# Attention logits over three PSUM banks, the third shared with the transposes

## The chip, the cores and the metric

The kernel runs on one core of one Trainium2 chip. The metric is the device time of one execution in microseconds (us); lower is better. The median of three runs of the kernel before is 2956.0 us (2955.72 to 2957.67).

## The reference

A decoder trunk of two layers over one sequence of 16 learned and 1024 given tokens (1040 rows of 1024 numbers): a state-space mixer and a gated feed-forward network (FFN), then attention and a second FFN. The change lies in the attention, which is of the stick-breaking kind, with 16 heads of 64:

```python
logits = jnp.einsum('bthd,bshd->bhts', q[:, t0:t1], k[:, :t1]).astype(jnp.float32) * scale
...
visible = s_idx < t_idx
log_keep = jnp.where(visible, jax.nn.log_sigmoid(-logits), 0.0)
later = lax.cumsum(log_keep, axis=3, reverse=True) - log_keep
log_w = jnp.where(visible, jax.nn.log_sigmoid(logits) + later, -jnp.inf)
w = jnp.exp(log_w).astype(v.dtype)
outs.append(jnp.einsum('bhts,bshd->bthd', w, v[:, :t1]))
```

Each weight is a sigmoid of its logit times the product of all sigmoids of the negated logits of later visible keys. The kernel computes that product directly, as a running product from right to left.

## The kernel before

The 16 heads go in eight pairs, p = 0 to 7. The 1040 tokens are nine chunks of 116 (the last has 112), and three chunks make a stretch of 348. A pair has 18 steps: step n is one chunk i of queries against one stretch jj of keys, for i = 0 to 8 and, within i, from the stretch that holds i down to the first. In the attention TensorE, VectorE, ScalarE and GpSimd run in the order in which the code is written; the code after it is ordered by a scheduler that works with simulated times.

One step, in the code's order:

- `weigh` (L1288): for both heads (a = 0, 1) a tile of logits `lg` in a PSUM bank, two products each (L1303). Then ScalarE makes from each tile the sigmoid of the negated logits, `kp` (L1306), and the plain sigmoid, `bt` (L1307), in the order kp0, bt0, kp1, bt1. A tile of logits is free after its `bt`. Where the stretch holds the query's own chunk (here jj = i // 3), GpSimd masks both (L1312). VectorE runs the product scan over `kp` (L1316) and multiplies it into `bt` (L1317).
- `place` (L1259): at steps 1, 3 and 9 the values of a stretch are turned on TensorE into a bank `pv` (L1267); VectorE evicts them to `v` (L1269), behind the scans of the step.
- `half` (L1209): half of a projection of 348 tokens, 12 products into a bank `pj` (L154 to L156). Steps 0 to 7 project for the pair itself, steps 8 to 17 for the next pair; the last pair has nothing there. Keys are evicted by VectorE (`k`, L1226), queries by ScalarE and VectorE (`qs`, L1250 and L1254), one step after their second half.
- pieces of the next weights' splitting (L1204 on ScalarE, L1205 on VectorE).
- `flush` (L1369): after every two chunks and after the last one of a pair the products with the values into a bank `po` (`values`, L1345; ScalarE evicts them as `o`, L1352), and in every step the transposes of the weights `bt` of three steps ago (`turn`): two banks `wT` (L1330), one for each head, evicted by ScalarE (L1334).

PSUM has eight banks, and four groups share them:

```python
def mm(self, s="mm"):
    return self.mp.tile([P, 512], F32, tag="mm", name=self.nm(s))
def sm(self, s="sm"):
    return self.sp.tile([P, 512], F32, tag="sm", name=self.nm(s))
def lg(self, s="lg"):
    return self.sp.tile([P, 512], F32, tag="lg", name=self.nm(s), bufs=LGB)
def ex(self, s="ex"):
    return self.sp.tile([P, 512], F32, tag="ex", name=self.nm(s), bufs=1)
```

`mm` has two banks (`pj`), `sm` three (`pv`, `wT`), `lg` two, `ex` one (`po`). A new tile gets a bank of its group when the tile that was in it has been read for the last time; within a group the allocator chooses the bank when the program is built. So before the change the tile of head a waits for `bt` of the same head in the step before.

## Time and profile before

| what | value |
|---|---|
| median of three runs | 2956.0 us |
| the profiled execution's own time | 2956.52 us |
| its span, first to last instruction | 2954.8 us |
| mean granted clock of TensorE | 0.988 |
| first and last logits of the attention | 1606.8 and 2130.4 us |
| products of logits (L1303) | 576, of 217 to 418 ns |

A profile row has the start and the length in us, engine, line, operation, tiles and shapes, and how many instructions it puts together; in brackets stands the idle time before it and the instruction that ended it. Products overlap on TensorE, so the pace is read from start to start. PE is TensorE, PEld its weight load, DVE VectorE, ACT ScalarE, POOL GpSimd.

### The profile page before, as it was taken

Reading aid. Unit: us, or ns where it says so; the run is one execution under the profiler, and the core shown is the slowest. Engines: PE = TensorE matmul, PEld = TensorE weight load, DVE = VectorE, ACT = ScalarE, POOL = GpSimd, SP = SyncE. Lnnn points to the kernel's source line nnn. Section 1 sums busy time; section 2 is a strip of 40 time slices with the busy share of each in tenths; the row PEclk is TensorE's granted clock in tenths of the full one; section 3 lists DMA queues with packets and bytes.
Section 4 is the critical chain, followed back from the end, with each engine's and each line's share of the span. In section 5 each row is a group of like instructions: output and inputs, shape, how many; then the busy total and the mean of one; then the engine's idle time right before and its main releaser. Section 6 shows DMA issues by size and latency. Waiting matters only on the chain.

```text
span 2954.8 us, 57105 instructions
## 1 busy us (share of the span) xinstructions
PE 2856.8 (97%) x21837; PEld 2723.3 (92%) x21837; DVE 2151.9 (73%) x4194; ACT 1616.9 (55%) x3302; POOL 962.6 (33%) x1088
## 2 busy tenths in 40 slices
PE   7999999989998999999999999999898999999998
PEld 4999898879998999999999999999798999999888
DVE  5686868885568565658986888888858656567895
ACT  4555545553236555555334888878726555555442
POOL 1253434440003666660002222222200666662000
PEclk9999999999999999999999999999999999999999
DMA  5233333324131222226242222222341222225331
GB/s 165 76 106 89 107 93 104 102 71 144 58 105 55 80 75 78 80 87 207 61 138 75 60 60 64 64 62 60 99 149 51 89 84 74 79 83 188 107 107 58
DMA packets 128962, 272.75 MB, mean 92 GB/s; under 512 B 15888, under 2 KB 59536, under 8 KB 128688
## 3 DMA queue, kind: packets, MB, share of 16 engines
q1 hardware_dynamic: 123376, 258.17, 27.7%
q10 hardware_dynamic: 4048, 6.36, 0.6%
q0 software_dynamic: 1264, 4.57, 0.4%
q8 instruction: 172, 2.82, 0.4%
q14 instruction: 102, 0.84, 0.1%
HBM read 200.93 MB, written 53.21 MB: 86 GB/s over the span
## 4 chain that ended last, share of the span: by engine, by line
PE 77%; DVE 12%; ACT 4%; issue 3%; DMA 2%; POOL 2%; SPq 0%; DVEq 0%; ACTq 0%; POOLq 0%
PE p L154 10%; PE p L155 10%; PE p L156 10%; PE acc L155 8%; PE acc L156 8%; PE acc L154 8%; PE pj L154 5%; PE pj L155 5%; PE pj L156 5%; PE po L1345 2%; PE lg L1303 2%; PE wT L1330 1%; DVE kp L1316 1%; DVE D L574 1%; ACT kp L1306 1%
## 5 line engine op out<-in xcount | busy, mean ns | idle before, releaser
L154 PE MATMUL pj<-uh,wh 128*128 128x348 f32 (+2 forms) x1536 | 506.9, 330 | 15.5 <-DVE qs L1254 7.2
L155 PE MATMUL pj<-ul,wh 128*128 128x348 f32 (+2 forms) x1536 | 498.7, 325 | 0.0
L156 PE MATMUL pj<-uh,wl 128*128 128x348 f32 (+2 forms) x1536 | 496.2, 323 | 0.0
L155 PE MATMUL p<-bl,fh 128*128 128x262 f32 (+1 forms) x1408 | 402.0, 286 | 4.1 <-DVE bl L837 4.1
L154 PE MATMUL p<-bh,fh 128*128 128x262 f32 (+1 forms) x1408 | 401.5, 286 | 3.2 <-ACT ft L937 2.3
L156 PE MATMUL p<-bh,fl 128*128 128x262 f32 (+1 forms) x1408 | 399.9, 285 | 0.2 <-DVE fl L890 0.2
L154 PEld LDWEIGHTS pj<-uh,wh 128*128 128x128 f32 x1536 | 291.8, 190 | 22.7 <-DVE qs L1254 9.3
L155 PE MATMUL p<-bl,wh 128*128 128x262 f32 (+1 forms) x1056 | 301.9, 286 | 6.7 <-DVE bl L837 6.7
L154 PE MATMUL p<-bh,wh 128*128 128x262 f32 (+1 forms) x1056 | 302.0, 286 | 3.4 <-ACT ft L937 1.8
L156 PE MATMUL p<-bh,wl 128*128 128x262 f32 (+1 forms) x1056 | 301.3, 286 | 0.0
L155 PEld LDWEIGHTS pj<-ul,wh 128*128 128x128 f32 x1536 | 292.5, 190 | 1.4 <-issue 0.5
L156 PEld LDWEIGHTS pj<-uh,wl 128*128 128x128 f32 x1536 | 291.6, 190 | 0.3 <-issue 0.2
L890 POOL TENSOR_TENSOR fl<-x,fh 128x1024 fp32r<-128x1024 f32 x80 | 192.6, 2408 | 251.8 <-ACT fh L889 251.8
L155 PEld LDWEIGHTS p<-bl,fh 128*128 128x128 f32 x1408 | 268.5, 191 | 6.0 <-DVE bl L837 5.7
L154 PEld LDWEIGHTS p<-bh,fh 128*128 128x128 f32 x1408 | 268.9, 191 | 4.6 <-ACT ft L937 2.8
L277 DVE SCALAR_TENSOR_TENSOR c<-p,params,c 128x260 f32<-128x260 f32 (+1 forms) x440 | 208.0, 482 | 89.0 <-ACT c L273 86.8
L156 PEld LDWEIGHTS p<-bh,fl 128*128 128x128 f32 x1408 | 267.7, 190 | 0.5 <-DVE fl L890 0.4
L940 DVE TENSOR_TENSOR p<-p,ft 128x262 f32<-128x262 f32 (+1 forms) x176 | 76.7, 437 | 215.5 <-ACT ft L937 123.8
L155 PE MATMUL acc<-gl,wh 128*128 128x260 f32 (+1 forms) x672 | 211.3, 320 | 0.1
L155 PEld LDWEIGHTS p<-bl,wh 128*128 128x128 f32 x1056 | 202.4, 192 | 7.7 <-DVE bl L837 7.7
L156 PE MATMUL acc<-gh,wl 128*128 128x260 f32 (+1 forms) x672 | 208.6, 320 | 0.0
L154 PEld LDWEIGHTS p<-bh,wh 128*128 128x128 f32 x1056 | 202.1, 192 | 4.3 <-ACT ft L937 2.5
(327 smaller groups left out, 7948.3 us busy)
## 6 DMA issues: line engine op xcount, KB each, us to landing
w<-in_w_up SPq DMA_DIRECT2D x88, 512.0 KB
w<-in_w_down SPq DMA_DIRECT2D x44, 512.0 KB
w<-in_w_in SPq DMA_DIRECT2D x40, 512.0 KB
E<-ea_d SPq DMA_DIRECT2D x32, 464.0 KB
D<-acs_d SPq DMA_DIRECT2D x32, 420.5 KB
g<-c SPq DMA_DIRECT2D x88, 130.0 KB
g<-c SPq DMA_DIRECT2D x88, 128.0 KB
b<-g SPq DMA_DIRECT2D x16, 520.0 KB
```

The lines of the kernel that those rows point to most:

```text
L154: mm(out, wh, uh, start=first, stop=False, skip_group_check=joins)
L155: mm(out, wh, ul, start=False, stop=False, skip_group_check=joins)
L156: mm(out, wl, uh, start=False, stop=last, skip_group_check=joins)
L277: nc.vector.scalar_tensor_tensor(to, ps[:, o + i : o + i + n], wcol(i), out, op0=ALU.mult, op1=ALU.add)
L574: nc.vector.tensor_scalar(dk[:, i], dk[:, i], self.cols[:n, 1, cc, h0 + i : h0 + i + 1], 0.0, op0=ALU.subtract, op1=ALU.min)
L890: tt(lo[:, :n], t, hi[:, :n].bitcast(F32), op=ALU.subtract)
L940: add = lambda o, x, y: tt(o[:, :N], x[:, :N], y[:, :N], op=ALU.add)
L1303: nc.tensor.matmul(ps[:nt, :m], part[:, c0 : c0 + nt], ks[a][:, s0 : s0 + m], start=x == 0, stop=x == 1)
L1306: nc.scalar.activation(kp[:nt, :m], ps[:nt, :m], AF.Sigmoid, scale=self.rt[2][:nt, i : i + 1])
L1316: nc.vector.tensor_tensor_scan(rev, rev, self.one[:nt].to_broadcast([nt, m + 1]), init, ALU.mult, ALU.mult)
L1330: nc.tensor.transpose(pt[:ns, x * CB : x * CB + nt], bt[a][:nt, x * CB : x * CB + ns], self.ident[:nt, :nt])
L1345: nc.tensor.matmul(po[64 * a : 64 * a + 64, w], v[: CH[c][1], c, 64 * a : 64 * a + 64], wt[a][: CH[c][1], c, :nt], start=x == 0, stop=x == ...
```

## The change

The tiles of logits take turns over a cycle of three calls, two of `lg` and one of `sm`. The cycle starts once for the attention; with 18 steps of two tiles each it stands alike in every pair. At steps 0, 3, 6 and so on both tiles are in `lg`; at steps 1, 4, 7, 10 and so on the first head's is in `sm`; at steps 2, 5, 8 and so on the second head's.

```diff
-            ps = self.lg()
+            ps = next(self.logits)("lg")
...
         turns, ready, wts, os, late, chores = [], [], {}, {}, [], []
+        self.logits = cycle((self.lg, self.lg, self.sm))
```

No instruction is added or taken away, and within the attention none changes its place on its engine. What changes is the tile that was in the bank before, and so what TensorE waits for. In the built program, from the second pair on:

| tile | waits for, before | waits for, after |
|---|---|---|
| second logits of a step | `bt1` of the step before | mostly `bt0` of the step before; at step 2 the first `wT` copy of step 1 |
| first logits of a step | `bt0` of the step before | tiles two steps back; at steps 4 and 10 the eviction of the `pv` of the step before |
| `pv` of step 1 | a `wT` copy of step 17 | the copy of the first `wT` of step 0 |
| `wT` | `wT` copies of the steps before, or `pv` | the same kind, or logits' `bt` |

TensorE from the last transposes of step 9 to the logits of step 10, in the fourth pair (`wT` transposes, `lg` logits, `qs` and `k` their operands):

```order
 L1330 MATMUL wT_21402<-ident,bt_21164 116x116 [waits Activation_49]
 L1330 MATMUL wT_21402<-ident,bt_21164 116x116 x2
-L1303 MATMUL lg_21410<-k_19989,qs_21061 116x348 [waits Activation_49]
+L1303 MATMUL lg_21410<-k_19989,qs_21061 116x348 [waits DVE_49,PE_49]
 L1303 MATMUL lg_21410<-k_19989,qs_21061 116x348
 L1303 MATMUL lg_21416<-k_19990,qs_21063 116x348 [waits Activation_49]
```

The first logits of step 10 stand where they stood, and wait for VectorE (the eviction of step 9's `pv`) instead of ScalarE.

TensorE at step 1 of the same pair, the logits and then `pv`:

```order
-L1303 MATMUL lg_20849<-k_19989,qs_20477 116x232 [waits Activation_49]
+L1303 MATMUL lg_20849<-k_19989,qs_20477 116x232 [waits PE_49]
 L1303 MATMUL lg_20849<-k_19989,qs_20477 116x232
 L1303 MATMUL lg_20855<-k_19990,qs_20479 116x232 [waits Activation_49]
 L1303 MATMUL lg_20855<-k_19990,qs_20479 116x232
-L1267 MATMUL pv_20874<-ident,v_20745 116x128 [waits PE_49]
+L1267 MATMUL pv_20874<-ident,v_20745 116x128 [waits PE_49,Activation_49]
```

The first logits no longer wait for ScalarE, and `pv` does.

Behind the attention the scheduler puts a few instructions of the second FFN's projection up in another order (some forty rows on TensorE, ten on VectorE and on ScalarE; SyncE and GpSimd keep theirs). TensorE there (`p` the sums, `bh` and `bl` the parts of the input, `fh` and `fl` of the weights):

```order
 L155 MATMUL p_27810<-bl_26764,fh_27734 128x258
 L156 MATMUL p_27810<-bh_26763,fl_27735 128x258
-L154 MATMUL p_27826<-bh_27392,fh_27734 128x258
-L155 MATMUL p_27826<-bl_27393,fh_27734 128x258
-L156 MATMUL p_27826<-bh_27392,fl_27735 128x258
-L154 MATMUL p_27826<-bh_27392,fh_27734 128x258
-L155 MATMUL p_27826<-bl_27393,fh_27734 128x258
 L154 MATMUL p_27635<-bh_27382,fh_26991 128x258
```

Five products of one sum moved behind a group of another sum; four of them now stand 12 rows later, behind that group, and the fifth some 50 rows later.

## The prediction

> **What bounds the kernel now.** I read the busy shares first, then the attention alone in the table by windows, then the waits of TensorE there, and last the timelines of one pair of heads around each wait. All steps below (0 to 17) are of the pair that starts at 1806.36 us; the pairs repeat every 67.4 us (step 0 of the next one stands at 1873.76).

> ```profile
> PE 2856.8 (97%) x21837; PEld 2723.3 (92%) x21837; DVE 2151.9 (73%) x4194; ACT 1616.9 (55%) x3302; POOL 962.6 (33%) x1088
> ...
> 1826.00:1879.00 53.00, 51.12 (x430) 48.47 (x430) 49.18 (x97) 45.08 (x128) 10.90 (x52) 1.00 0.27 73
> ...
> PE lg L1303 <- ACT bt L1307: 8.5, 24, 0.6
> PE pj L154 <- DVE qs L1254: 7.2, 7, 1.0
> ```

> TensorE is the kernel's bound as a whole. In the attention the table's columns (length; busy time of PE, PEld, DVE, ACT, POOL; granted clock) show two engines near their limit from step 4 to the next step 0: PE 51.1 and DVE 49.2 of 53 us. The last two rows are what TensorE waits for: the logits for ScalarE's second sigmoid (8.5 us in 24 waits), and once in each of seven pairs a projection for VectorE's `qs` (1.0 us). Only the first kind is a wait for a bank of the logits.

> VectorE has no room between these two points. It starts when ScalarE hands it step 4, runs on without a pause, and pauses again only before step 1 of the next pair:

> ```profile
> 1825.92 0.94 DVE L1316 TENSOR_TENSOR_SCAN kp<-kp,kp,one 116x349 f32<-116x349 f32 x1 [2.61 <-ACT kp L1306]
> ...
> 1846.86 0.61 DVE L1269 TENSOR_TENSOR v<-pv,rt 116x256 f32<-116x256 f32 x2
> ...
> 1848.86 0.94 DVE L1316 TENSOR_TENSOR_SCAN kp<-kp,kp,one 116x349 f32<-116x349 f32 x1
> ...
> 1866.96 1.07 DVE L1254 TENSOR_TENSOR qs<-pj,qs 64x348 fp32r<-64x348 f32 x2
> ```

> So the times of VectorE's rows between step 4 and step 16 are fixed relative to step 4, whatever TensorE gains in between. That decides which gains are kept.

> **What the change removes.** Three waits for logits' banks per pair, at steps 0, 8 and 12. TensorE's rows, each stalled place with one of the same width that isn't stalled (steps 3, 2 and 1):

> ```profile
> 1806.36 0.39 PE L1303 MATMUL lg<-k,qs 128*116 128x116 f32 x2
> 1807.15 0.41 PE L1303 MATMUL lg<-k,qs 128*116 128x116 f32 x2 [0.40 <-ACT bt L1307]
> 1807.40 0.38 PE L154 MATMUL pj<-uh,wh 128*128 128x348 f32 x1
> ...
> 1813.13 0.66 PE L1303 MATMUL lg<-k,qs 128*116 128x232 f32 x4
> 1813.63 0.49 PE L1267 MATMUL pv<-ident,v 128*116 128x128 f32 x3
> ...
> 1816.37 0.88 PE L1303 MATMUL lg<-k,qs 128*116 128x348 f32 x4
> 1817.08 0.32 PE L154 MATMUL pj<-uh,wh 128*128 128x344 f32 x1
> ...
> 1819.46 0.60 PE L1303 MATMUL lg<-k,qs 128*116 128x116 f32 x4
> 1819.90 0.52 PE L1267 MATMUL pv<-ident,v 128*116 128x128 f32 x3
> ...
> 1836.86 1.25 PE L1303 MATMUL lg<-k,qs 128*116 128x348 f32 x4
> 1837.94 0.32 PE L154 MATMUL pj<-uh,wh 128*128 128x348 f32 x1
> ...
> 1845.03 0.87 PE L1303 MATMUL lg<-k,qs 128*116 128x348 f32 x4
> ...
> 1851.33 0.45 PE L1303 MATMUL lg<-k,qs 128*116 128x232 f32 x2
> 1852.10 0.47 PE L1303 MATMUL lg<-k,qs 128*116 128x232 f32 x2 [0.32 <-ACT bt L1307]
> 1852.41 0.33 PE L154 MATMUL pj<-uh,wh 128*128 128x348 f32 x1
> ...
> 1866.18 0.87 PE L1303 MATMUL lg<-k,qs 128*112 128x348 f32 x4
> 1868.09 0.42 PE L154 MATMUL pj<-uh,wh 128*128 128x348 f32 x1 [1.03 <-DVE qs L1254]
> ```

> From the first product of the logits to what follows: step 0 takes 1.04 us where step 3 takes 0.44, loss 0.60; step 12 takes 1.08 where step 1 takes 0.50, loss 0.58; step 8 takes 1.08 where step 2 takes 0.71, loss 0.37. With the change the second tile of such a step waits for the first tile's sigmoids of the step before, and no longer for the second's. ScalarE's rows for step 0:

> ```profile
> 1805.65 0.56 ACT L1307 ACTIVATE bt<-lg,rt 112x348 f32<-112x348 f32 x1
> ...
> 1806.52 0.58 ACT L1307 ACTIVATE bt<-lg,rt 112x348 f32<-112x348 f32 x1
> ...
> 1813.11 0.51 ACT L1334 ACTIVATE wt<-wT 116x224 f32<-116x224 f32 x2
> ...
> 1816.41 0.45 ACT L1334 ACTIVATE wt<-wT 116x336 f32<-116x336 f32 x1
> ```

> The first ends at 1806.21, before step 0 begins; the second, at 1807.10, is today's wait. All three waits go.

> **What it adds.** The logits now hold banks that `pv` and `wT` held, and TensorE takes its work in order, so everything behind a late tile waits with it.
> (a) Step 1: `pv` needs the bank of the first `wT` of step 0, which the third ScalarE row frees at 1813.62, 0.01 us ahead of `pv`'s 1813.63. From the end of `qs` (1868.03) to the product that waits for it (1868.09) a hand-over takes 0.06, so 0.05 to 0.1 is lost.
> (b) Step 2: the second logits' tile needs the first `wT` of step 1, free at 1816.86 (last ScalarE row); it would start after two of the step's four products, a little past half of their 0.71 us since the first one waits for its weights, at about 1816.76 (an estimate). Loss 0.15 to 0.25. I take 0.3 for (a) and (b); ends 0 and 0.6.
> (c) Step 10: the first logits' tile takes the bank of step 9's `pv`. VectorE empties that at 1847.47 (1846.86 + 0.61), because the eviction stands in its queue behind both scans of step 9. The logits want it at 1845.03. They start at 1847.53, 2.50 late. Before the change the next `wT` had this bank and came after the whole half projection.

> **What of it stays on the path.** VectorE's end at 1847.47 doesn't move, so what step 8 gains (0.37) is only waited away at step 10. Behind step 10 TensorE is 2.50 late; step 12 gives back 0.58; at step 16 it used to wait for `qs` anyway: its projection would come at 1866.18 + 0.71 = 1866.89 and comes at 1868.09, so 1.20 is absorbed, and 0.10 more since products after a wait start slower. Left: 2.50 − 0.58 − 1.20 − 0.10 = +0.62. From step 0 to step 4 TensorE alone sets the pace (VectorE's 2.61 us pause), so the 0.60 of step 0 is kept and (a) and (b) are paid in full. A pair costs +0.62 − 0.60 + 0.30 = +0.32, and seven of them +2.2 us. The eighth has no projections after step 7; there TensorE has room:

> ```profile
> 2108.00:2139.00 31.00, 23.06 (x230) 17.82 (x226) 28.35 (x46) 26.13 (x73) 7.27 (x28) 1.00 0.48 167
> ```

> VectorE is busy 28.4 of 31 us with short hand-overs, and its last scan sets the end, so a late bank there costs nothing.

> VectorE itself must not be held up by the late logits of step 10: their two products end about 0.57 after 1847.53, a sigmoid of 0.55 follows, so the scan's input is there at 1848.7, and the scan stands at 1848.86. Cover of 0.1 to 0.2; if it is gone, each 0.1 costs 0.7 us over seven pairs.

> **The clock.** The wait at step 10 leaves TensorE idle for 2.6 to 2.8 us (0.37 earlier by step 8, less the drain of the last transposes). What such pauses did elsewhere in this kernel, by windows, and the pace at the lower clock:

> ```profile
> 485.00:488.40 3.40, 0.49 (x3) 0.23 (x3) 2.08 (x4) 3.37 (x6) 0.00 (x0) 1.00 0.61 248
> 488.40:491.80 3.40, 3.40 (x22) 3.40 (x22) 3.40 (x9) 2.17 (x4) 1.30 (x1) 1.00 0.14 53
> ...
> 2265.30:2268.50 3.20, 1.17 (x10) 0.96 (x8) 3.20 (x7) 1.36 (x4) 0.00 (x0) 1.00 0.00 0
> 2268.60:2272.00 3.40, 2.99 (x12) 2.69 (x12) 3.40 (x9) 0.72 (x2) 0.00 (x0) 0.50 0.00 0
> 1867.00:1870.40 3.40, 2.37 (x17) 2.29 (x17) 3.18 (x5) 1.64 (x4) 0.10 (x1) 1.00 0.44 104
> ...
> 1592.14 0.49 PE L156 MATMUL pj<-uh,wl 128*128 128x348 f32 x1
> 1592.43 0.48 PE L154 MATMUL pj<-uh,wh 128*128 128x348 f32 x1
> ...
> 1593.08 0.32 PE L154 MATMUL pj<-uh,wh 128*128 128x348 f32 x1
> 1593.24 0.32 PE L155 MATMUL pj<-ul,wh 128*128 128x348 f32 x1
> ```

> A pause of 2.9 us left the clock at 1.00, one of 2.0 us within 3.2 was followed by 3.4 us at 0.50, and step 16's 1.0 us did nothing. At half clock products of 348 columns follow each other at 0.29 us instead of 0.16, so 3.4 us lose 3.4 × (1 − 0.16/0.29) = 1.5 us. The new wait lies nearest to the second of these, so I take the halving in five of seven pairs: +7.5 us. Ends: none, and all seven with one more tenth each for the slower restart, 11.2. At that point nothing absorbs it, since `qs` is by then no longer waited for.

> **The sum.** +2.2 + 7.5 = +9.7 us on the profiled execution's 2956.5 (span 2954.8): 2966.2. The median shown is 2956.0, 0.5 lower, so I say 2966. The second FFN's projection up, where the scheduler put some products in another order, can add or take a halving or so:

> ```profile
> 2230.00:2280.00 50.00, 42.22 (x275) 39.02 (x274) 49.67 (x121) 29.88 (x68) 0.22 (x2) 0.90 0.13 43
> ```

> There TensorE idles 7.8 of 50 us behind VectorE and the clock is already at 0.90; I set ±1.5 us and count it as nothing. The forecast's own range is 2961 to 2972.

> **The rivals.** A measurement of this kernel can't tell changes within 0.2% (5.9 us) from none.
> - No difference: the clock stays full through the new wait, as it did at 485 us. Then the pairs' +2.2 is all, 2958; with one or two halvings still below 2962. [...] The rows at 2265 to 2272 speak against it, since there 1.17 of 3.20 us were busy and the clock still halved. Chance 0.2.
> - Faster: `pv`'s bank at step 10 is free in time after all, and the three waits are gone with nothing in their place: 7 × (0.60 + 0.58 + 0.37) = 10.9 us, 2945. For it: 24 of the waits are for just these banks. [...] Against it: VectorE would have to evict `pv` 2.4 us earlier, and it has no pause in which to catch up; and even then step 16's wait for `qs` would take back steps 8 and 12, and leave 4 us. It decides from an eviction before 1845 us. Chance 0.07.
> - Slower still: the late logits of step 10 hold up VectorE's scans, `qs` is late too, and step 16 absorbs nothing. A pair then costs 2.50 − 0.60 + 0.30 = 2.2, with the halvings 7 × 2.2 + 7.5 = 23: 2979. It decides from a scan of step 10 after 1848.9, in this pair's time. Chance 0.1.

> **How the numbers follow.** The forecast has 0.63, the rivals 0.2, 0.07 and 0.1. Slower is the forecast and the last rival, 0.73; the same 0.2; faster 0.07. The range of 2957 to 2974 takes in the forecast, the rival without the clock and the lower part of the last.

> **What the profile after would show.** Right: no wait of `lg` for `bt` at steps 0, 8 and 12 before the last pair; a new row, `lg` for `DVE v`, about seven times and 2.4 to 2.8 us each; the wait of `pj` for `qs` gone; a granted clock below 1.00 in the attention; VectorE without a longer pause between steps 4 and 16. Wrong: `lg` waiting for `v` less than 1 us, the clock at 1.00 throughout the attention, or VectorE pausing at step 10.

## The result, and the profile after

The changed kernel is slower: 2964.21 us, median of nine runs (2956.11 to 2970.92), against 2956.0 us of the kernel before on the same chip, nine runs (2952.62 to 2958.34). The ratio is 1.0029, with a 95% interval of 1.0021 to 1.0038. The profiled execution took 2961.24 us, its span 2959.5 us, 3.0 us below its median, and its mean granted clock is 0.988.

The page's first line shows almost nothing of this; PE is at 2856.8 us before and 2855.2 after:

```profile
PE 2855.2 (96%) x21837; PEld 2724.5 (92%) x21837; DVE 2155.6 (73%) x4194; ACT 1617.1 (55%) x3302; POOL 957.9 (32%) x1088
```

The waits of TensorE in the attention show it (total us, times, longest). The 24 waits of logits for `bt` (8.5 us) and the seven for `qs` (7.2 us) are gone, but for one of 0.3; in their place stand seven waits for VectorE's eviction of `v`, 2.4 to 2.8 us each:

```profile
PE lg L1303 <- DVE v L1269: 18.8, 7, 2.8
...
PE lg L1303 <- ACT bt L1307: 0.3, 1, 0.3
```

Eleven of the 24 (3.9 us) lay in the last pair. In the seven pairs ahead of it the listed waits grew from 12.7 to 19.7 us, but their sum is not the account of the loss: each of the seven pairs has the new wait, and they did not lose alike. Where the loss is, the table by pairs tells. Each row is one pair of heads, from its first logits to those of the next; columns are length, busy times of PE, PEld, DVE, ACT and POOL, granted clock, DMA share, GB/s. First the kernel before (its second and its fifth pair, and the sum of seven), then the one after (all seven):

```profile
1671.43:1738.93 67.50, 65.54 (x568) 62.32 (x568) 57.08 (x113) 53.88 (x156) 16.03 (x72) 1.00 0.22 61
...
1873.76:1941.23 67.47, 65.60 (x570) 62.42 (x569) 57.03 (x113) 53.82 (x156) 16.01 (x72) 1.00 0.22 60
...
sum 469.20, PE 455.73 PEld 433.96 DVE 396.86 ACT 374.34 POOL 111.34; mean PE 65.10 PEld 61.99 DVE 56.69 ACT 53.48 POOL 15.91
```

```profile
1604.80:1671.32 66.52, 63.24 (x480) 61.35 (x478) 55.48 (x121) 52.13 (x144) 15.23 (x72) 0.97 0.24 67
1671.32:1740.67 69.35, 66.60 (x571) 63.89 (x569) 57.51 (x114) 54.26 (x157) 15.81 (x72) 0.98 0.21 59
1740.67:1808.47 67.80, 65.04 (x570) 62.32 (x569) 56.83 (x112) 53.45 (x155) 15.02 (x72) 1.00 0.21 60
1808.47:1877.62 69.15, 66.41 (x571) 63.70 (x569) 57.37 (x114) 54.12 (x157) 15.90 (x72) 0.98 0.21 59
1877.62:1945.41 67.79, 65.05 (x570) 62.35 (x569) 56.85 (x113) 53.50 (x156) 15.02 (x72) 1.00 0.21 60
1945.41:2013.19 67.78, 65.06 (x570) 62.36 (x569) 57.13 (x113) 53.77 (x156) 15.02 (x72) 1.00 0.21 60
2013.19:2082.36 69.17, 66.41 (x571) 63.69 (x569) 57.38 (x114) 54.19 (x157) 15.81 (x72) 0.98 0.20 53
sum 477.56, PE 457.80 PEld 439.66 DVE 398.54 ACT 375.43 POOL 107.81; mean PE 65.40 PEld 62.81 DVE 56.93 ACT 53.63 POOL 15.40
```

The seven pairs grew by 477.56 − 469.20 = 8.36 us. They fall into two kinds, and the clock column tells them apart. The three at 1.00 are 0.32 to 0.39 us longer than the same pairs before. The four at 0.97 or 0.98 are 1.75 to 1.92 longer. On average the four lost 1.46 more than the three, so seven tenths of the loss, 4 × 1.46 = 5.8 of 8.4 us, came with a lower clock.

One wait and what follows it, in the fourth pair, which has the half clock. VectorE's scan of step 4, its eviction of `v` and the scan of step 10; then TensorE's logits at steps 0, 2, 8, 10, 12 and 16 with the projection behind them:

```profile
1827.77 0.94 DVE L1316 TENSOR_TENSOR_SCAN kp<-kp,kp,one 116x349 f32<-116x349 f32 x1 [2.83 <-ACT kp L1306]
...
1848.71 0.61 DVE L1269 TENSOR_TENSOR v<-pv,rt 116x256 f32<-116x256 f32 x2
...
1851.07 0.94 DVE L1316 TENSOR_TENSOR_SCAN kp<-kp,kp,one 116x349 f32<-116x349 f32 x1 [0.27 <-ACT kp L1306]
```

```profile
1808.47 0.60 PE L1303 MATMUL lg<-k,qs 128*116 128x116 f32 x4
1808.91 0.38 PE L154 MATMUL pj<-uh,wh 128*128 128x348 f32 x1
...
1817.97 1.12 PE L1303 MATMUL lg<-k,qs 128*116 128x348 f32 x4
1818.93 0.32 PE L154 MATMUL pj<-uh,wh 128*128 128x344 f32 x1
...
1838.70 0.87 PE L1303 MATMUL lg<-k,qs 128*116 128x348 f32 x4
1839.41 0.32 PE L154 MATMUL pj<-uh,wh 128*128 128x348 f32 x1
...
1849.47 1.48 PE L1303 MATMUL lg<-k,qs 128*116 128x348 f32 x4 [2.74 <-DVE v L1269]
1850.75 0.49 PE L154 MATMUL pj<-uh,wh 128*128 128x348 f32 x1
1851.04 0.49 PE L155 MATMUL pj<-ul,wh 128*128 128x348 f32 x1
...
1857.11 0.67 PE L1303 MATMUL lg<-k,qs 128*116 128x232 f32 x4
1857.61 0.33 PE L154 MATMUL pj<-uh,wh 128*128 128x348 f32 x1
...
1871.32 0.87 PE L1303 MATMUL lg<-k,qs 128*112 128x348 f32 x4
1872.03 0.32 PE L154 MATMUL pj<-uh,wh 128*128 128x348 f32 x1
```

From the logits to what follows them: steps 0, 8, 12 and 16 now take 0.44, 0.71, 0.50 and 0.71 us, where they took 1.04, 1.08, 1.08 and 1.91: no stall is left there. Step 2 takes 0.96 instead of 0.71, and step 10 comes 2.74 us after TensorE had run dry. Behind it products follow at 0.29 us instead of 0.16, at a granted clock of 0.50.

### The profile page after: what moved, and what is told of

It is laid out like the page before. It is cut to its first block, busy times and chain, and to the rows that moved or that the text cites. A ratio compares the mean times of both kernels' runs of the same rounds, so it can differ in the third digit from the quotient of the medians.

```text
span 2959.5 us, 57115 instructions
## 1 busy us (share of the span) xinstructions
PE 2855.2 (96%) x21837; PEld 2724.5 (92%) x21837; DVE 2155.6 (73%) x4194; ACT 1617.1 (55%) x3302; POOL 957.9 (32%) x1088
## 4 chain that ended last, share of the span: by engine, by line
PE 82%; DVE 8%; issue 3%; ACT 2%; POOL 2%; DMA 1%; SPq 0%; ACTq 0%; DVEq 0%; POOLq 0%
PE p L154 9%; PE p L156 9%; PE p L155 9%; PE acc L155 8%; PE acc L156 8%; PE acc L154 8%; PE pj L154 6%; PE pj L155 6%; PE pj L156 6%; PE lg L1303 3%; PE po L1345 2%; PE wT L1330 2%; DVE D L574 1%; PE ms L816 1%; DVE bl L837 1%
## 5 line engine op out<-in xcount | busy, mean ns | idle before, releaser
L154 PE MATMUL pj<-uh,wh 128*128 128x348 f32 (+2 forms) x1536 | 507.0, 330 | 8.8 <-ACT bk L605 6.5
L155 PE MATMUL pj<-ul,wh 128*128 128x348 f32 (+2 forms) x1536 | 500.2, 326 | 0.0
L156 PE MATMUL pj<-uh,wl 128*128 128x348 f32 (+2 forms) x1536 | 497.4, 324 | 0.1
L155 PE MATMUL p<-bl,fh 128*128 128x262 f32 (+1 forms) x1408 | 401.8, 286 | 3.6 <-DVE bl L837 3.6
L154 PE MATMUL p<-bh,fh 128*128 128x262 f32 (+1 forms) x1408 | 400.7, 286 | 4.5 <-ACT ft L937 2.9
L156 PE MATMUL p<-bh,fl 128*128 128x262 f32 (+1 forms) x1408 | 399.8, 285 | 0.8 <-DVE fl L890 0.8
L155 PE MATMUL p<-bl,wh 128*128 128x262 f32 (+1 forms) x1056 | 300.1, 284 | 7.2 <-DVE bl L837 7.2
L154 PEld LDWEIGHTS pj<-uh,wh 128*128 128x128 f32 x1536 | 293.4, 191 | 13.4 <-issue 4.6
L154 PE MATMUL p<-bh,wh 128*128 128x262 f32 (+1 forms) x1056 | 300.6, 285 | 3.6 <-ACT bh L836 2.3
L156 PE MATMUL p<-bh,wl 128*128 128x262 f32 (+1 forms) x1056 | 299.6, 284 | 0.0
L155 PEld LDWEIGHTS pj<-ul,wh 128*128 128x128 f32 x1536 | 293.8, 191 | 1.4 <-issue 0.5
L156 PEld LDWEIGHTS pj<-uh,wl 128*128 128x128 f32 x1536 | 293.3, 191 | 0.7 <-POOL wl L1195 0.4
L154 PEld LDWEIGHTS p<-bh,fh 128*128 128x128 f32 x1408 | 268.3, 191 | 6.2 <-ACT ft L937 3.5
L155 PEld LDWEIGHTS p<-bl,fh 128*128 128x128 f32 x1408 | 267.9, 190 | 5.6 <-DVE bl L837 5.3
L156 PEld LDWEIGHTS p<-bh,fl 128*128 128x128 f32 x1408 | 267.7, 190 | 1.1 <-DVE fl L890 1.0
L155 PE MATMUL acc<-gl,wh 128*128 128x260 f32 (+1 forms) x672 | 211.2, 320 | 0.4 <-DVE gl L1038 0.4
L155 PEld LDWEIGHTS p<-bl,wh 128*128 128x128 f32 x1056 | 201.0, 190 | 8.2 <-DVE bl L837 8.2
L156 PE MATMUL acc<-gh,wl 128*128 128x260 f32 (+1 forms) x672 | 208.4, 319 | 0.0
L154 PEld LDWEIGHTS p<-bh,wh 128*128 128x128 f32 x1056 | 200.7, 190 | 4.4 <-ACT bh L836 2.7
```

The costliest lines, as they stand in the source:

```text
L154: mm(out, wh, uh, start=first, stop=False, skip_group_check=joins)
L155: mm(out, wh, ul, start=False, stop=False, skip_group_check=joins)
L156: mm(out, wl, uh, start=False, stop=last, skip_group_check=joins)
```

## Experiments

**The theory**: VectorE sets the pace behind step 4. Its eviction of step 9's `v` is late, and the borrowed bank makes TensorE wait for it. A pair pays a few tenths for that, and the larger part is the half clock that followed in four of the seven pairs. **Rivals**: the third bank itself, in the other steps, costs the time; or TensorE loses what it waits, in proportion, and the clock is only a companion.

Each median below was measured beside runs of the kernel before on the same chip, but not all rows on one chip, so the ratios are what to compare. "Seven pairs" is the sum row of the same table as above.

| kernel | us | ratio to before, 95% | seven pairs, us |
|---|---|---|---|
| before | 2955 to 2956 | 1 | 469.20 |
| changed | 2964.21 | 1.0029 (1.0021 to 1.0038) | 477.56 |
| changed, once more | 2964.52 | 1.0028 (1.0017 to 1.0040) | 477.32 |
| only step 10 borrows | 2958.24 | 1.0012 (1.0003 to 1.0021) | 475.19 |
| all but step 10 borrow | 2952.19 | 0.9992 (0.9983 to 1.0000) | 467.39 |
| half projection ahead of step 10 | 2954.48 | 1.0000 (0.9991 to 1.0009) | 468.83 |
| useless work in the pause | 2956.42 | 1.0004 (0.9995 to 1.0013) | 471.51 |
| `v` of step 9 earlier | 2953.45 | 0.9993 (0.9984 to 1.0002) | 467.28 |
| `v` of step 9 on ScalarE | 2947.15, 2948.43 | 0.9974 (0.9963 to 0.9986), 0.9980 (0.9971 to 0.9989) | 463.34 |
| the same, all but step 10 borrow | 2948.29 | 0.9978 (0.9969 to 0.9987) | 463.27 |
| the same, two banks | 2950.82 | 0.9987 (0.9978 to 0.9996) | 465.67 |

**Only step 10's first logits borrow a bank** (the kernel before, with one tile changed):

```diff
-            ps = self.lg()
+            ps = self.sm("lg") if (i, jj, a) == (6, 1, 0) else self.lg()
```

> The kernel before, and only the first logits of step 10 take a bank of the transposes' group (the one that pv of step 9 held). Theory A (the loss is the wait of step 10 for VectorE, paid mainly through a halved clock): TensorE waits there 2.2 to 2.5 us in seven pairs; without halving a pair costs about nothing (step 16 absorbs 1.2, the old waits of steps 12 and 0 shrink because TensorE arrives later), each halving costs 1.5 us, so 2960 to 2965 with the time following the number of halvings. Theory B (the clock hardly matters; the loss is the small waits of steps 1 and 2 and the products put in another order behind the attention): 2955 to 2958, since none of that is here.

Measured: 2958.24 us, ratio 1.0012; slower than before, but 1.8 us under the theory's range, and just above the rival's. The trace decides between them. Its waits, and two of its pairs:

```profile
PE lg L1303 <- DVE v L1269: 16.1, 7, 2.3
```

```profile
1807.16:1874.65 67.49, 65.00 (x570) 62.38 (x569) 56.73 (x112) 53.62 (x155) 14.66 (x72) 1.00 0.21 61
1874.65:1943.68 69.03, 66.55 (x570) 63.91 (x569) 57.49 (x114) 54.22 (x157) 15.31 (x72) 0.98 0.22 59
```

A later pair at full clock costs about 0.1 more than before (67.49 against 67.40 to 67.47), about nothing, as expected, where the prediction's sum has +0.62 behind step 4. Behind a late step 17 the old wait at step 0 of the next pair, 0.60 us, is used up as well: in the seven pairs the listed waits for `bt` fell from 13 (4.6 us) to 5 (0.9 us). In the first two pairs that wait was being used up, and they got 0.4 longer each. What is left is the clock: three of the seven pairs at 0.98, 1.5 to 1.6 longer than their neighbours. The wait is 2.3 instead of 2.7 us, because step 8 still stalls here. So the one tile alone makes the kernel slower, and most of its loss is clock (4.8 of 6.0 us in the seven pairs of this execution). The expected range was too high: on the 2954.8 us beside it, its lower end takes between three and four halvings of 1.5 us, and this execution has three.

**All tiles but that one borrow** (the changed kernel):

```diff
-            ps = next(self.logits)("lg")
+            bank = next(self.logits)
+            ps = (self.lg if (i, jj, a) == (6, 1, 0) else bank)("lg")
```

> The changed kernel, but the first logits of step 10 come from the two banks of the logits. Theory A: no wait for pv's bank, clock 1.00 through the attention; steps 8 and 12 gain 0.95 us and step 16 takes it back waiting for qs; step 0 gains 0.60, steps 1 and 2 lose 0.3: minus 0.3 us a pair, 2954 (2952 to 2956). Theory B: the waits of steps 1 and 2 and the order behind the attention are still here, so 2960 or more.

Measured: 2952.19 us, ratio 0.9992, against 1.0029 with that tile.

```profile
PE pj L154 <- DVE qs L1254: 10.1, 14, 1.0
PE wT L1331 <- DVE v L1269: 2.1, 7, 0.9
```

```profile
1802.53:1869.65 67.12, 65.49 (x570) 62.15 (x569) 56.94 (x113) 53.79 (x156) 16.39 (x72) 1.00 0.22 61
```

The whole loss hangs on this one tile in 36. Step 4 borrows a bank from `pv` in the same way and doesn't wait: in the changed kernel's fourth pair VectorE has emptied it at 1824.94 us, and the logits start at 1826.13. The other borrowed banks gain 0.26 a pair (469.20 to 467.39 over seven), and no more, although the waits for `bt` are all gone: the waits for `qs` doubled to 14 and took the gains of steps 8 and 12. That is the bound by VectorE behind step 4.

**Step 10's half projection ahead of its logits**, so that TensorE has 1.9 us of work while it would wait:

```diff
+                first_half = now[-1].half(*halves[-1, n]) if n == 10 and -1 in now else []
...
-                todo, late = late, []
+                todo, late = late, first_half
...
-                    if (own, n) in halves:
+                    if (own, n) in halves and n != 10:
```

> The changed kernel, with the half projection of step 10 (12 products, 1.9 us) ahead of that step's logits, so that TensorE works while VectorE still holds the bank. Theory A: the wait shrinks from 2.7 to 0.6 to 1.0 us, the clock stays at 1.00, step 16 waits for qs again: minus 0.3 us a pair, 2954 (2952 to 2956). Theory B: the logits come no earlier, so no gain against the changed kernel's 2964.

Measured: 2954.48 us, ratio 1.0000. The wait shrinks to 0.8 us, the clock stays at 1.00 in all seven pairs:

```profile
PE lg L1303 <- DVE v L1269: 5.4, 7, 0.8
```

The expected gain of 0.3 us a pair didn't come (468.83 against 469.20 over seven pairs), nor did step 16's wait for `qs`, which is listed once, with 0.4 us; in their place stand fourteen waits for ScalarE of 0.3 us at most. The experiment can't part "the wait is shorter" from "the clock stays up", which the next one does.

**Useless work in the pause**: 18 transposes of 128 columns ahead of step 10's logits, into a bank that is free there. The wait for VectorE stays, TensorE has more to do.

```diff
+                if n == 10 and p + 1 < PAIRS:
+                    fill = self.ex("fill")
+                    for _ in range(18):
+                        self.nc.tensor.transpose(fill[:, :P], self.ident, self.ident)
```

> The changed kernel, with 18 useless transposes of 128 columns on TensorE ahead of the logits of step 10 in seven pairs (126 products, about 11 us of added work; their result is read by nobody). Theory A: they lie in the pause, which still ends with VectorE's eviction, but is now split or shortened to about 1 us, so the clock stays at 1.00: 2956 + 7 x 0.36 = 2958.5 (2957 to 2960), faster than without the added work. Theory B: they fill a pause that costs no clock, so no change from 2964, or slower.

Measured: 2956.42 us, ratio 1.0004, with 126 more instructions on TensorE than the changed kernel; that is 0.6 us under the expected range. Step 10 in its fourth pair, and that pair:

```profile
1843.78 2.13 PE L1401 MATMUL fill<-ident 128*128 128x128 f32 x18
1846.68 0.86 PE L1303 MATMUL lg<-k,qs 128*116 128x348 f32 x4 [0.76 <-DVE v L1269]
```

```profile
1805.69:1873.46 67.77, 67.01 (x588) 64.28 (x587) 57.08 (x113) 53.73 (x156) 15.07 (x72) 1.00 0.22 60
```

Every pair from the second on now takes what the changed kernel's pairs at full clock take (67.73 to 67.80 against 67.78 to 67.80), and none has a lower clock. The logits wait for the same eviction and start no earlier: 41.0 us behind step 0 in both kernels. This separates the two parts: about 0.3 us a pair for the changed waits, the rest of the loss, 477.56 − 471.51 = 6.0 us, for the half clock.

**The changed kernel once more**, to see whether the same pairs are hit.

> The changed kernel once more, beside the variants on their chip. Both theories expect some 9 us more than before (ratio 1.002 to 1.004). They differ on which of the seven waits at step 10 are followed by a half clock. Theory of position (the clock is set by windows of 3.41 us that follow one another, each by how long TensorE idled in the one before): the seven pauses of 2.7 to 2.8 us again fall into two kinds, those with over 2.2 us inside one window are followed by 3.4 us at half clock, those split more evenly (no part over 1.9 us) are not; which pairs these are changes from run to run. Rival (the length of the pause decides): all seven are followed by a half clock, or none.

Measured: 2964.52 us, ratio 1.0028. Its seven pauses are again 2.4 to 2.7 us in the trace, and four pairs were halved, but others than in the first profile: there the first, second, fourth and seventh, here the first, second, third and sixth. Two of its rows, the fourth pair (halved before) and the sixth:

```profile
1808.24:1876.02 67.78, 65.05 (x570) 62.34 (x569) 56.78 (x112) 53.35 (x155) 15.07 (x72) 1.00 0.21 60
...
1943.77:2012.88 69.11, 66.41 (x571) 63.72 (x569) 57.26 (x114) 54.00 (x157) 15.92 (x72) 0.98 0.21 59
```

What decides at these pauses is where they lie. In the profiles before and after all changes of the clock stand at whole multiples of 3.41 us from each other (after, those at 302.76 and 2118.65 us are 532 such steps apart), so the time can be cut into such windows. Three waits of the first profile, each with the window that holds most of it and the next one (second, third and fourth pair). They are cut to within 0.1 us, hence 0.99 and 0.51:

```profile
1709.13:1712.54 3.41, 0.66 (x6) 0.47 (x5) 3.20 (x13) 1.21 (x4) 0.59 (x6) 0.99 0.00 0
1712.54:1715.95 3.41, 3.41 (x13) 3.41 (x13) 3.14 (x8) 2.83 (x8) 0.10 (x1) 0.51 0.35 100
...
1777.40:1780.81 3.41, 1.51 (x12) 1.27 (x11) 3.07 (x10) 2.31 (x8) 1.68 (x8) 1.00 0.00 2
1780.81:1784.22 3.41, 2.54 (x16) 2.57 (x17) 3.28 (x10) 1.96 (x5) 0.10 (x1) 1.00 0.07 13
...
1845.60:1849.00 3.40, 1.13 (x10) 0.89 (x8) 3.06 (x11) 1.91 (x7) 1.28 (x8) 1.00 0.00 0
1849.00:1852.40 3.40, 2.93 (x10) 2.96 (x11) 3.00 (x9) 1.99 (x5) 0.10 (x1) 0.50 0.17 31
```

PE busy 0.66 or 1.13 us in a window: the next runs at half clock. Busy 1.51, with 0.9 us of the same pause falling into the next window: full clock. In the first profile the seven pauses have at most 2.22, 2.75, 1.82, 2.27, 1.38, 1.85 and 2.36 us of their length inside one window. Over all fourteen pauses of the two profiles those with 1.94 us or more inside one window were followed by a half clock, and those with at most 1.85 were not, as expected. The seven pauses of the run in which only step 10 borrows fall the same way: 2.29 us or more inside one window, half clock; 1.68 or less, full clock. In the run with useless work four of the seven pauses, without that work, would have had 2.35 to 2.76 us inside one window (an estimate from where they lie in its trace), so it is the work that kept the clock up there, and not where the pauses fell. The limit doesn't hold for all of the kernel: elsewhere in the first profile windows with PE busy 1.69 and 2.15 of 3.41 us (from 299.33 and 2115.24 us) were followed by a half clock too, and what counts there besides idle time isn't shown. The ends of products are modelled, so all these idle times are estimates. The rival by the length of the pause alone falls: pauses of 2.74 us went both ways. And the 1.13 us of work in the window from 1845.60 us did not keep the clock up behind it.

**`v` of step 9 evicted earlier**: its transposes and eviction ahead of step 9's logits and scans. The wait stays, only shorter.

```diff
+                if n == 9:
+                    now[0].place()
                 bt = self.weigh(i, jj, now[0].qd[i // 3], now[0].ks, prev, pool)
...
-                now[0].place()
+                if n != 9:
+                    now[0].place()
```

> The changed kernel, with step 9's transposes of v and VectorE's eviction of them ahead of step 9's logits and scans. TensorE still waits at step 10 for the eviction, but it comes 1.38 us earlier (from 1847.33, where the scans stood, instead of 1848.71), so that the wait is 1.3 to 1.5 us instead of 2.75. Theory A (the loss is the half clock, and it takes more than 1.6 us of idling in a window): no half clock in the attention before the last pair, pairs 67.1 us as in the kernel without step 10's wait, ratio 0.9990 to 1.0000. Rival B (every wait at this place costs, in proportion to its length): half of the changed kernel's loss stays, ratio 1.0013 to 1.002.

Measured: 2953.45 us, ratio 0.9993.

```profile
PE lg L1303 <- DVE v L1269: 8.7, 7, 1.3
PE pj L154 <- DVE qs L1254: 3.3, 7, 0.8
```

```profile
1803.76:1870.90 67.14, 65.41 (x571) 62.40 (x569) 56.92 (x113) 53.77 (x156) 16.49 (x72) 1.00 0.22 61
```

Half of the wait costs nothing: the pair is as short as where step 10 doesn't borrow (67.12), because the 1.3 us are taken off the waits behind it (3.3 us for `qs` in all, where it was 10.1). A cost in proportion to the wait is excluded.

**`v` of step 9 evicted by ScalarE** (three copies with a scale, 0.93 us in the trace, in place of two multiplications on VectorE):

```diff
+                        if j == 2:
+                            for c in range(x, y):
+                                nc.scalar.activation(v[:m, 3 * j + c], pv[:m, c * P : c * P + P], AF.Copy, scale=self.rt[0][:m, 3 * j + c : 3 * j + c + 1])
+                            continue
                         nc.vector.tensor_tensor(v[:m, 3 * j + x : 3 * j + y], ...
```

> The changed kernel, with step 9's v evicted by ScalarE (three copies with a scale instead of two multiplications on VectorE). Theory A (behind step 4 VectorE sets the pace of a pair, and the late bank is its backlog): the wait at step 10 falls under 1 us, the clock stays full, VectorE has 0.6 us less to do up to step 16, so a pair takes 66.5 us instead of 67.43: 7 x 0.9 = 6.5 us less than before, ratio 0.9972 to 0.9984. Rival B (ScalarE, busy 45 of 53 us in this stretch, is as full, and its three copies push the sigmoids back): pairs of 67.1 or more, ratio 0.999 or above.

Measured: 2947.15 us, ratio 0.9974, faster than both kernels.

```profile
PE pj L154 <- DVE qs L1254: 6.9, 7, 1.1
```

```profile
1801.15:1867.71 66.56, 65.60 (x570) 62.31 (x569) 56.35 (x111) 54.35 (x159) 16.40 (x72) 1.00 0.22 61
```

The wait at step 10 is gone, and the pair is 0.56 shorter than without the borrowed bank (67.12), close to the 0.6 that VectorE no longer does. The wait for `qs` is still there: VectorE still sets the pace. ScalarE had room for the copies: it is busy 54.35 of the pair's 66.56 us.

**Two controls of it.** With step 10 in its own banks:

> As the one before, and step 10's first logits take one of their own two banks. Theory A: the wait at step 10 was already short there, so nothing is left to gain: within 0.05% of the one before. Rival B: ScalarE's copies come late enough that the borrowed bank still costs about 0.5 us a pair: 3 to 4 us faster than the one before.

Measured: 2948.29 us, and 463.27 us for the seven pairs against 463.34. No difference, as the theory has it. With two banks for the logits, as before the change, and a second measurement with three beside it:

> The kernel before, two banks for the logits, with only step 9's v evicted by ScalarE. It tells what the third bank is worth once VectorE has the 0.6 us less. Theory A (behind step 4 VectorE sets the pace, and only step 0's wait lies in TensorE's own stretch): a pair takes 67.43 - 0.61 = 66.8 us, 4.3 us less in seven pairs, ratio 0.9982 to 0.999, some 3 to 4 us slower than the same eviction with three banks. Rival B (the third bank is worth nothing, the eviction is all): the time of the version with three banks, ratio 0.997 to 0.998.

> Three banks and step 9's v on ScalarE, beside the same eviction with two banks. Theory A: 2947 to 2949 us, 3 to 4 us faster than with two banks. Rival B: no difference between the two.

Measured: 2950.82 us with two banks, 2948.43 with three; intervals of the ratios 0.9978 to 0.9996 and 0.9971 to 0.9989 overlap. The seven pairs differ by 465.67 − 463.34 = 2.3 us (with three banks, those of the first measurement), the medians by 2.4. The third bank seems worth 2.4 us here, less than the 3 to 4 expected. The times alone don't settle it, but in the two traces every pair from the second on is longer with two banks (66.83 to 67.26 us against 66.54 to 66.63).

## Why the prediction was right

It said 2966 us; the median is 2964.21. Its steps, against the trace:

- **Steps 0, 8, 12, 16**: the three stalls removed and the wait for `qs` absorbed, as in the rows above. Step 10's pause is 2.74 us, where 2.6 to 2.8 were forecast.
- **(a) and (b)**: 0.3 taken for both. Step 2 loses 0.96 − 0.71 = 0.25. Step 1, from its logits to the projection behind `pv`, takes 0.84 us instead of 0.74, loss 0.10. Step 0 to step 4 comes out at −0.30, where −0.60 + 0.25 + 0.10 gives −0.25.
- **VectorE's times fixed from step 4**: the eviction stood 20.94 us behind step 4's scan before (1846.86 − 1825.92), and stands 20.94 behind it after (1848.71 − 1827.77). TensorE's 0.37 from step 8 was waited away, as said.
- **The size of a pair at full clock**: +0.62 behind step 4, −0.30 ahead of it. The fifth pair, cut at step 4, after and before:

```profile
1877.62:1895.30 17.68, 17.68 (x189) 16.54 (x188) 11.83 (x24) 9.54 (x32) 6.91 (x26) 1.00 0.05 11
1895.30:1945.41 50.11, 47.37 (x383) 45.81 (x383) 45.02 (x89) 43.95 (x125) 8.11 (x46) 1.00 0.27 77
```

```profile
1873.76:1891.74 17.98, 17.57 (x189) 16.66 (x188) 12.49 (x25) 10.25 (x33) 7.15 (x27) 1.00 0.05 11
1891.74:1941.23 49.49, 48.03 (x383) 45.76 (x383) 44.54 (x88) 43.57 (x124) 8.86 (x45) 1.00 0.29 78
```

  That is −0.30 and +0.62, sum +0.32, the prediction's figures.
- **The clock**: five halvings of 1.5 us were forecast; both profiles have four, of about 1.4 to 1.5 (69.15 − 67.79 = 1.36; by the pairs' differences 1.46). This is the term most off, by 1.7 us. The prediction asked how long a pause is and took the count from the nearest of its rows; it did not ask where the pauses would fall. That five came near four is partly luck. The row that it set against a halving fits the position too: in windows counted from the half clock at 2138.89 us in the kernel before, the 2.9 us at 485 us lay across a boundary, 1.5 in one window and 1.4 in the next, and the clock stayed up:

```profile
483.41:486.82 3.41, 1.88 (x12) 1.60 (x10) 1.84 (x8) 2.10 (x3) 0.00 (x0) 1.00 0.94 384
486.82:490.23 3.41, 2.02 (x13) 2.06 (x14) 3.34 (x10) 3.40 (x7) 0.00 (x0) 1.00 0.28 111
```

- **The spread**: the changed kernel's runs spread over 15 us, those before over 6, and the mean granted clock goes with the time: 0.991 in the run of 2956.11 us, 0.986 in the median one, 0.985 in the one of 2970.92. Both profiled executions lie below their medians, by 3.0 and 5.5 us, so how many halvings the median one has isn't shown.
- **VectorE not held up**: in pairs at full clock it wasn't. In the halved fourth pair step 10's scan came 0.27 late and a later one 0.88 (at 1863.87 us), so the cover of 0.1 to 0.2 was gone there, and the sign of being wrong, VectorE pausing at step 10, shows in that pair. It follows the half clock and added nothing that can be seen: the pair is 1.36 longer than one at full clock, and 1.5 were counted for a halving alone.
- **Outside the pairs**, nothing was counted. In the profiles the last pair, up to the first product behind its values, is 1.5 us shorter than before (65.36 against 66.85), because the kernel before had a half clock at its end: the last 36 products with the values took 3.14 us there and 1.95 after. The changed kernel's own half clock in that pair, 6.8 us from 2118.65 on, cost nothing: VectorE's last scan starts 61.3 us behind the pair's first logits in both, as the prediction has it for the eighth pair. And the attention starts 2.0 us earlier (1604.80 against 1606.83) on unchanged code. Together these offset 3.5 us of the 8.4, so the profiled execution lost 4.7 us (2961.24 − 2956.52), half of the 9.7 forecast, while the medians lost 8.2. So it is partly luck, too, that the median came within 2 us of the forecast.

Of the rivals, "no difference" fell with the lower clock in four pairs of seven. Its premise, that the clock stays full through the new wait, doesn't hold here: four pauses of 2.4 to 2.8 us were followed by a half clock. "Faster" gave 4 us for a bank that is free in time; where all but step 10 borrow, nearly that case was built, and gave 2954.8 − 2952.2 = 2.6 us (the first is the kernel before on that chip). "VectorE held up" shows only in the halved pair, by the times above, and did not set the pace.

## What to carry to other kernels

Before an accumulator borrows a bank, ask which engine releases it and how far behind that engine runs at that step: one late release in 36 tiles undid the gain of the others and cost 8 us more. The stalls removed at steps 8 and 12, ahead of an engine that already sets the pace, came back as waits for that engine (where all but step 10 borrow, 14 for `qs` instead of seven), so moving 0.6 us of work off VectorE gained more than the banks, 3.5 us over the seven pairs with two banks against 1.8. And a pause of TensorE cost twice here, once as time (about 0.3 us a pair for the changed waits) and once as clock (1.4 to 1.5 us a halving); where it couldn't be removed, shortening it (to 1.3 or 0.8 us) or filling it, even with useless work, took the second part away.
